# First attention's scores by pairs of heads, the products with the keys' remainder on 64 rows

## The chip, the core and the metric

One kernel launch on one core of a Trainium2 chip. The metric is the device time of one execution, in microseconds (us); times are medians of several runs, and the profile is of one further execution. PE is TensorE, PEld its weight loads, DVE is VectorE, ACT ScalarE, POOL GpSimd, SP SyncE, which only issues transfers here.

## What is computed

Two transformer blocks one after the other on 512 tokens of width 1024. The change touches the attention of the first block's second layer. It has 16 query heads of 64 columns, 4 key/value heads (so 4 query heads share one key head), a window of 128 tokens to either side, 256 context tokens that every query sees, and a sink logit. Cut to what matters:

```python
def block_fn(args):                       # one block of 128 queries
    i, qb = args
    kb = lax.dynamic_slice_in_dim(k_pad, i * BLOCK, 3 * BLOCK, axis=1)
    vb = lax.dynamic_slice_in_dim(v_pad, i * BLOCK, 3 * BLOCK, axis=1)
    ...
    s_band = jnp.einsum('bqhgd,bkhd->bhgqk', qb, kb)          # window, masked
    s_ctx = jnp.einsum('bqhgd,bkhd->bhgqk', qb, kc)           # context
    p = jax.nn.softmax(jnp.concatenate([s_band, s_ctx, s_sink_lat], axis=-1), axis=-1)
    o = einsum(p_band, vb) + einsum(p_ctx, vc)
```

Everything is float32. The kernel gets near it with matmuls in the type fp32r, which takes one pass where float32 takes two (a float32 matmul stands in the trace as two instructions): each operand is split into a rounded part ("hi", names ending in h) and the remainder ("lo", ending in l), and a product is the sum hi·hi + lo·hi + hi·lo.

## The kernel before

The program is built by a tile framework that gets the operations in the order in which the Python code emits them, with priorities, and runs a list scheduler over them: the order on each engine is the scheduler's, chosen by what it holds to be ready, not the order of emission. So a Python loop sets what there is to do and the dependences, and only loosely the order.

A linear layer (`mm3`, lines 155 to 165; L161, L163 and L165 are its three matmuls) loads 128x128 of the weights and streams up to 512 tokens. These are most of the run. The first attention (`attend`, `queries`, `wo`, from line 840) lies at 975 to 1174 us of 2372. Group g (0 to 3) is one key head with its four query heads, block b (0 to 3) is 128 queries; `attend(g, b)` is called 16 times. Between the calls stand the query projection of the next group (`queries`, L161 to L165 with xh, xl) and the output projection of the group before (`wo`, the same lines with oh, ol).

In `attend` each head i of the four does this:

- The stationary operand is q, 128 rows by 128 queries. A head has only 64 columns, so q holds the head twice: hi on one half of the rows and lo on the other. Even heads have hi on rows 0 to 63, odd heads on rows 64 to 127 (L856 writes hi, L859 computes lo, which a transfer moves to the other half). The keys' hi part kh[g] stands on both halves of the rows (L812 and a transfer), and so does the remainder kl[g] (L813).
- So one matmul q·kh (L887) gives hi·hi + lo·hi, and a second one, q·kl (L888), adds hi·lo and also lo·lo.
- The scores go to a PSUM tile `sc` of 1024 columns, of which there are two. There are two spans: the window's keys (384 columns for blocks 1 and 2, 256 for blocks 0 and 3) and the 256 of the context. So a head has four matmuls, and all heads 64 x 4 = 256: 128 on L887 and 128 on L888.
- DVE adds the mask and takes the maximum (L890), which frees the `sc` tile; ACT takes the exponential (L891); when all four heads are done DVE computes the reciprocal of the sum (L894 to L897) and POOL scales the rows (L899).
- For each block of 128 keys PE transposes the four heads' weights (L905, tile `aux`), ACT copies them (L907), and PE multiplies by the values (L909, tile `po`). L909 writes 64 partitions per matmul, two of them side by side in the array.

The form of a PE instruction in the trace gives the piece of the array that it uses, rows * columns: 128\*128 is the whole array, 128\*64 has half the columns (L909), 64\*128 half the rows.

Of the kernel before, what the change touches and what calls it, by code (L numbers as in the profile page):

```python
# [11 lines left out]
AF = mybir.ActivationFunctionType  # L12
ALU = mybir.AluOpType
# [44 lines left out]
def _build(ctx, tc, ins, out, stop, dbg):  # L58
    nc = tc.nc
    pe, act, dve, pool, sp = nc.tensor, nc.scalar, nc.vector, nc.gpsimd, nc.sync  # L60
# [8 lines left out]
    cur = B()  # L69
    cur.bufs, cur.tags, cur.done, cur.st = {}, {}, [0] * KT, None  # L70

    @contextmanager
    def sub(name, attr, side="left"):

        with tc.tile_pool(name=name, bufs=1, side=side, reuse_waits="tile") as p:
            old = getattr(cur, attr, None)
            setattr(cur, attr, p)
            yield
            setattr(cur, attr, old)

    @contextmanager
    def banks(name, **tags):

        with tc.tile_pool(name=name, bufs=1, space=PSUM, reuse_waits="tile") as p:
            old = cur.tags
            cur.tags = {t: list(l) for t, l in old.items()}
            for t, n in tags.items():
                cur.tags[t] = [(p, n)] * n + cur.tags.get(t, [])
            cur.turn = {}
            yield  # L90
            cur.tags = old

    def ps(cols=512, tag="mm", parts=128):
        n = cur.turn.get(tag, 0)
        cur.turn[tag] = n + 1
        p, bufs = cur.tags[tag][n % len(cur.tags[tag])]
        return p.tile([parts, cols], F32, tag=tag, bufs=bufs, name=tag)

    def wk(cols, tag, bufs=1, dt=F32, parts=128, first=False):

        p, bufs = cur.sm, cur.bufs.get(tag, bufs)
        if cur.st and tag in ("cv", "u"):
            n = cur.turn.get(tag, 0)
            cur.turn[tag] = n + 1
            p, bufs = (cur.st, 2) if first or n % bufs < 2 else (p, bufs - 2)
        return p.tile([parts, cols], dt, tag=tag, bufs=bufs, name=tag)
# [15 lines left out]
    def V(name, i=0, n=1):  # L122
        o, c = _VOFF[name]
        assert i + n <= c
        return vec[:, o + i : o + i + n]
# [4 lines left out]
    def load_unit(src, u, cols=2048):  # L130
        raw = cur.wp.tile([128, 2048], F32, tag="raw", bufs=cur.raw, name="raw")
        sp.dma_start(out=raw[:, :cols], in_=src[u][:, :cols])
        return raw

    def split_w(raw, h, p=None):
        part = raw[:, h * 1024 : (h + 1) * 1024]
        cur.nw += 1
        if p is None and cur.early_w and cur.nw % (cur.w + 1) == 0:
            p = cur.wa
        p, n = (cur.wp, cur.w) if p is None else (p, 1)  # L140
        hi = p.tile([128, 1024], F32R, tag="wh", bufs=n, name="wh")
        lo = p.tile([128, 1024], F32R, tag="wl", bufs=n, name="wl")
        act.activation(out=hi, in_=part, func=AF.Copy)  # L143
        dve.tensor_tensor(out=lo, in0=part, in1=hi, op=ALU.subtract)  # L144
        return hi, lo
# [9 lines left out]
    def mm3(pieces, w, xs, first, last, mcol):  # L155

        whi, wlo = w
        xhi, xlo = xs
        c = slice(mcol, mcol + 128)
        for p, s in pieces:  # L160
            pe.matmul(p, whi[:, c], xhi[:, s], start=first, stop=False)  # L161
        for p, s in pieces:
            pe.matmul(p, whi[:, c], xlo[:, s], start=False, stop=False)  # L163
        for p, s in pieces:
            pe.matmul(p, wlo[:, c], xhi[:, s], start=False, stop=last)  # L165
# [268 lines left out]
    with sub("a_x", "xp"), sub("a_w", "wp"), sub("a_s", "sm"):  # L434
# [13 lines left out]
        for k in range(KT):  # L448
            q = wk(TOK, "prod", 2)
# [11 lines left out]
        r = wk(8, "rs", 2)  # L461
# [303 lines left out]
    kh = [wk(TOK, f"kh{g}", dt=F32R) for g in range(4)]  # L765
    kl = [wk(TOK, f"kl{g}", dt=F32R) for g in range(4)]
# [5 lines left out]
    nsink = wk(16, "nsink")  # L772
# [67 lines left out]
    qs, ob, qp = {}, {}, [cur.sm, None]  # L840
# [32 lines left out]
    with sub("c_b", "oa"), sub("c_a", "sm", "right"), banks("c_p1", mm=1), banks("c_p2", sc=2), banks("c_p0", po=1), banks("c_p3", aux=2):  # L873
        qp[1] = cur.sm
        def attend(g, b):
            blocks = [t for t in (b - 1, b, b + 1) if 0 <= t < 4]
            nb = 128 * len(blocks)
            W = nb + 256
            mk = mask[:, 0:640] if len(blocks) == 3 else mask[:, 128:640] if b == 0 else mask[:, 640:1152]
            c = slice(b * 128, (b + 1) * 128)  # L880
            n4, l4 = wk(4, "n4", 3), wk(4, "l4", 3)
            P = []
            for i in range(4):
                q = qs[4 * g + i][:, c]
                sc = ps(1024, tag="sc")
                for dst, src in ((sc[:, 512 - nb : 512], slice(blocks[0] * 128, blocks[0] * 128 + nb)), (sc[:, 512:768], slice(512, 768))):
                    pe.matmul(dst, q, kh[g][:, src], start=True, stop=False)  # L887
                    cur.mark = pe.matmul(dst, q, kl[g][:, src], start=False, stop=True)  # L888
                s = wk(640, "s", 8)
                dve.tensor_tensor_reduce(out=s[:, :W], in0=sc[:, 512 - nb : 768], in1=mk, scale=1.0, scalar=nsink[:, 4 * g + i : 4 * g + i + 1], op0=ALU.add, op1=ALU.min, accum_out=n4[:, i : i + 1])  # L890
                act.activation(out=s[:, :W], in_=s[:, :W], func=AF.Exp, scale=-1.0, bias=n4[:, i : i + 1], accum_out=l4[:, i : i + 1])  # L891
                P.append(s)
            e4 = wk(4, "e4", 3)
            dve.tensor_tensor(out=e4, in0=V("sink1", 4 * g, 4), in1=n4, op=ALU.add)  # L894
            act.activation(out=e4, in_=e4, func=AF.Exp)
            dve.tensor_tensor(out=l4, in0=l4, in1=e4, op=ALU.add)
            dve.reciprocal(out=l4, in_=l4)  # L897
            for i in range(4):
                pool.tensor_tensor(out=P[i][:, :W], in0=P[i][:, :W], in1=l4[:, i : i + 1].to_broadcast([128, W]), op=ALU.mult)  # L899
            po = ps(256, tag="po")  # L900
            keys = blocks + [4, 5]
            for n, t in enumerate(keys):
                pt = ps(512, tag="aux")
                for i in range(4):
                    pe.transpose(pt[:, i * 128 : (i + 1) * 128], P[i // 2 + i % 2 * 2][:, n * 128 : (n + 1) * 128], ident)  # L905
                p = wk(512, "p", 3)
                act.copy(out=p, in_=pt)  # L907
                for e in range(2):
                    pe.matmul(po[64 * e : 64 * e + 64], va[:, t, g], p[:, 256 * e : 256 * e + 256], start=n == 0, stop=n == len(keys) - 1)  # L909
            if b == 0:  # L910
                ob[g] = [cur.oa.tile([128, 1024], F32R, tag=n, bufs=3, name=n).rearrange("p (j t) -> p j t", j=2) for n in ("oh", "ol")]
            o = po.rearrange("p (j t) -> p j t", j=2)
            oh, ol = [x[:, :, c] for x in ob[g]]
            act.activation(out=oh, in_=o, func=AF.Copy)
            dve.tensor_tensor(out=ol, in0=o, in1=oh, op=ALU.subtract)

        def wo(g, cols=512, tags=("mm",)):
            raw = load_unit(ins["wo"], g)
            ws = [split_w(raw, 0), split_w(raw, 1)]
            for c0 in range(0, 512, cols):  # L920
                for m in range(KT):
                    t = tags[m % len(tags)]
                    p = (ps(512) if t == "mm" else ps(1024, tag="sc"))[:, 0:cols]
                    for i in range(2):
                        mm3([(p, slice(c0, c0 + cols))], ws[i], [x[:, i] for x in ob[g]], i == 0, i == 1, m * 128)
                    dve.scalar_tensor_tensor(out=hl[m][:, c0 : c0 + cols], in0=p, scalar=mod[1][:, 16 + m, 0:1], in1=hl[m][:, c0 : c0 + cols], op0=ALU.mult, op1=ALU.add)
                    cur.done[m] = tc.cur_priority

        for g in range(4):
            for b in range(4):  # L930
                attend(g, b)
                if b == QB and g < 3:
                    queries(g + 1)
                if (g, b) in WOP:
                    with tc.issue_after(cur.mark.ins) if WOI else ExitStack():
                        wo(WOP.index((g, b)))
        wo(3, 256, ("sc", "mm", "sc"))
# [151 lines left out]
    bias = wa(6 * 256, "bias").rearrange("p (h j) -> p h j", h=6)  # L1089
# [182 lines left out]
    with sub("e_x", "xp"), sub("e_w", "wp"), sub("e_t", "sm"):  # L1272
# [34 lines left out]
        for n, (name, i) in enumerate(order):  # L1307
# [12 lines left out]
            if name in ("l", "r", "k", "v"):  # L1320
                shifted(u, {"r": 0, "k": 3, "v": 6, "l": 9}[name] + i, lora if name == "l" else rkv[name][i])
                if n == PREPN:
# [8 lines left out]
                    m4k, eye64, pair = rc[0], rc[1][:, 0:64], rc[1][:, 64:192]  # L1331
# [384 lines left out]
```

## Time and profile before

| | |
|---|---|
| median of 3 runs | 2374.22 us (2371.76 to 2375.54) |
| the profiled execution | 2373.74 us, its span 2372.0 us |
| mean granted TensorE clock | 0.987 |
| PE busy | 2279.0 us, 96% of the span |
| DVE, ACT, POOL busy | 69%, 40%, 7% |
| first attention (975 to 1163 us): PE busy | 178.6 of 188 us |
| its score matmuls L887 and L888 | 256 instructions |

A matmul's duration in the trace includes its passage through the array, which lies over the next matmul's; so what a matmul costs in a row of matmuls is read from start to start, and the busy time of a group is more than what it costs. Where a row says x2 or x4, consecutive instructions of one kind are merged.

### The profile page before, as it was taken

The page shows a single profiled execution, that of the slowest core. Times are in us where ns is not written, and L with a number is a line of the kernel's source. Part 1 is how long each engine was busy: PE and PEld are TensorE (multiplying, and loading weights), DVE is VectorE, ACT ScalarE, POOL GpSimd, SP SyncE. Part 2 cuts the span into 40 slices and gives each one's busy share as a digit, 9 for nine tenths or more (in the row PEclk, how much of TensorE's full clock was granted, in tenths as well). Part 3 has the DMA queues.
Part 4 walks back from the last instruction along what each step waited for, and adds up shares of the span by engine and source line. Part 5 has one row for each costly group of instructions (what it writes and reads, how often), then busy time and mean ns, then how long its engine had stood idle before and what let it go on. Part 6 is the DMA issues. An engine that isn't in the chain of part 4 may idle for free.

```text
span 2372.0 us, 34287 instructions
## 1 busy us (share of the span) xinstructions
PE 2279.0 (96%) x13910; PEld 1885.8 (80%) x13910; DVE 1644.5 (69%) x2634; ACT 942.7 (40%) x1616; POOL 170.9 (7%) x246
## 2 busy tenths in 40 slices
PE   5999899999999999899999999998989999999999
PEld 2777588888888888766789999987768786788887
DVE  4889769867677768666687777676645546767666
ACT  3222633223332235566653433355633323433332
POOL 0000000000000000344300000001431100000000
PEclk8999999999999999999999999999999999999999
DMA  8455323323233211421132322222200002232221
GB/s 314 168 206 172 139 115 116 124 99 107 90 128 112 98 54 55 129 68 36 54 118 78 124 74 106 72 73 68 66 23 23 5 28 105 87 106 90 89 89 54
DMA packets 51385, 229.02 MB, mean 97 GB/s; under 512 B 6395, under 2 KB 11164, under 8 KB 32796
## 3 DMA queue, kind: packets, MB, share of 16 engines
q1 hardware_dynamic: 51228, 226.84, 27.8%
q8 instruction: 109, 1.79, 0.3%
q14 instruction: 48, 0.39, 0.1%
HBM read 213.84 MB, written 6.68 MB: 93 GB/s over the span
## 4 chain that ended last, share of the span: by engine, by line
PE 88%; DVE 5%; ACT 3%; DMA 2%; issue 1%; POOL 0%; SPq 0%; DVEq 0%; ACTq 0%; POOLq 0%
PE mm L161 23%; PE mm L163 23%; PE mm L165 23%; PE po L909 1%; PE aux L905 1%; PE mm L576 1%; PE rw L1436 1%; PE rw L1430 1%; PE rw L1424 1%; DMA raw<-in_ada 1%; PE aux L370 1%; PE sc L887 1%; PE mm L783 1%; PE sc L888 1%; PE aux L402 1%
## 5 line engine op out<-in xcount | busy, mean ns | idle before, releaser
L161 PE MATMUL mm<-xh,wh 128*128 128x512 f32 (+2 forms) x2336 | 658.4, 338 | 15.2 <-ACT xh L479 4.7
L163 PE MATMUL mm<-xl,wh 128*128 128x512 f32 (+2 forms) x2336 | 660.9, 337 | 3.1 <-DVE xl L219 2.1
L165 PE MATMUL mm<-xh,wl 128*128 128x512 f32 (+2 forms) x2336 | 659.7, 337 | 1.9 <-DVE wl L144 1.9
L143 ACT ACTIVATE wh<-raw 128x1024 fp32r<-128x1024 f32 x263 | 274.8, 1057 | 543.3 <-PE mm L163 491.9
L161 PEld LDWEIGHTS mm<-xh,wh 128*128 128x128 f32 x2336 | 409.5, 190 | 70.5 <-ACT xh L479 6.8
L163 PEld LDWEIGHTS mm<-xl,wh 128*128 128x128 f32 x2336 | 410.8, 190 | 55.5 <-DVE xl L219 3.1
L165 PEld LDWEIGHTS mm<-xh,wl 128*128 128x128 f32 x2336 | 410.7, 190 | 49.2 <-DVE wl L144 2.8
L144 DVE TENSOR_TENSOR wl<-raw,wh 128x1024 fp32r<-128x1024 f32 x263 | 324.2, 1242 | 44.5 <-ACT wh L143 40.0
L161 PE MATMUL mm<-gh,wh 128*128 128x512 f32 (+1 forms) x704 | 253.7, 368 | 2.2 <-ACT gh L288 2.0
L163 PE MATMUL mm<-gl,wh 128*128 128x512 f32 (+1 forms) x704 | 254.8, 368 | 0.0
L165 PE MATMUL mm<-gh,wl 128*128 128x512 f32 x704 | 254.0, 367 | 0.0
L249 DVE TENSOR_TENSOR u<-mm,R 128x256 f32<-128x256 f32 x88 | 37.5, 426 | 178.5 <-PE mm L165 176.7
L161 PEld LDWEIGHTS mm<-gh,wh 128*128 128x128 f32 x704 | 131.3, 188 | 26.1 <-ACT gh L288 2.4
L165 PEld LDWEIGHTS mm<-gh,wl 128*128 128x128 f32 x704 | 131.3, 189 | 23.4
L163 PEld LDWEIGHTS mm<-gl,wh 128*128 128x128 f32 x704 | 131.3, 189 | 23.0 <-DVE gl L289 0.3
L310 DVE SCALAR_TENSOR_TENSOR hl<-mm,mod,hl 128x512 f32<-128x512 f32 x176 | 131.3, 747 | 21.1 <-PE mm L165 20.5
L288 ACT ACTIVATE gh<-cv 128x512 fp32r<-128x512 f32 (+1 forms) x66 | 46.5, 705 | 243.0 <-DVE cv L286 243.0
L271 DVE SCALAR_TENSOR_TENSOR cv<-u,vec,cv 128x512 f32<-128x512 f32 (+1 forms) x132 | 110.4, 837 | 9.9 <-ACT cv L262 9.2
L553 DVE SCALAR_TENSOR_TENSOR accp<-v,dwt,accp 128x798 f32<-128x798 f32 (+2 forms) x118 | 113.9, 975 | 2.6
L272 DVE SCALAR_TENSOR_TENSOR cv<-u,vec,cv 128x512 f32<-128x512 f32 (+1 forms) x132 | 110.6, 839 | 3.1
L284 ACT ACTIVATE cv<-cv 128x512 f32<-128x512 f32 (+1 forms) x66 | 46.4, 704 | 118.2 <-DVE cv L272 118.0
L396 DVE SCALAR_TENSOR_TENSOR ac<-ra,sc,ac 128x512 f32<-128x512 f32 x112 | 81.8, 744 | 1.4 <-DMA ra<-in_ada 1.4
(470 smaller groups left out, 3092.2 us busy)
## 6 DMA issues: line engine op xcount, KB each, us to landing
raw<-in_up SPq DMA_DIRECT2D x63, 1024.0 KB, 4.9
raw<-in_dn SPq DMA_DIRECT2D x33, 1024.0 KB, 4.8
raw<-in_ada SPq DMA_DIRECT2D x24, 1024.0 KB, 6.3
ra<-in_ada SPq DMA_DIRECT2D x48, 512.0 KB, 3.6
raw<-in_pw SPq DMA_DIRECT2D x12, 1024.0 KB, 6.2
S<-vd SPq DMA_DIRECT2D x28, 407.0 KB, 5.0
raw<-in_w_in SPq DMA_DIRECT2D x17, 512.0 KB, 3.5
raw<-in_qkv SPq DMA_DIRECT2D x6, 1024.0 KB, 5.0
```

The lines of the kernel that those rows point to most:

```text
L143: act.activation(out=hi, in_=part, func=AF.Copy)
L144: dve.tensor_tensor(out=lo, in0=part, in1=hi, op=ALU.subtract)
L161: pe.matmul(p, whi[:, c], xhi[:, s], start=first, stop=False)
L163: pe.matmul(p, whi[:, c], xlo[:, s], start=False, stop=False)
L165: pe.matmul(p, wlo[:, c], xhi[:, s], start=False, stop=last)
L271: dve.scalar_tensor_tensor(out=cv[:, 0:CW], in0=u[:, 0:CW], scalar=wv[0], in1=cv[:, 0:CW], op0=ALU.mult, op1=ALU.add)
L272: dve.scalar_tensor_tensor(out=cv[:, 0:CW], in0=u[:, 2 : 2 + CW], scalar=wv[2], in1=cv[:, 0:CW], op0=ALU.mult, op1=ALU.add)
L284: act.activation(out=ca[:, 0:CW], in_=ca[:, 0:CW], func=AF.Silu)
L288: act.activation(out=gh[:, 0:CW], in_=cb[:, 0:CW], func=AF.Copy)
L310: dve.scalar_tensor_tensor(out=hs, in0=p, scalar=g2[i][:, m : m + 1], in1=hs, op0=ALU.mult, op1=ALU.add)
L396: dve.scalar_tensor_tensor(out=a, in0=t[:, q, :], scalar=sc2[:, k, n : n + 1], in1=a, op0=ALU.mult, op1=ALU.add)
L553: dve.scalar_tensor_tensor(out=acc[:, a:b], in0=x, scalar=w, in1=acc[:, a:b], op0=ALU.mult, op1=ALU.add)
```

## The change

The heads are taken by pairs (0, 1) and (2, 3). For a pair, the code emits the four matmuls with kh as before, over all 128 rows. Then it emits the four with kl, span by span, the two heads' alternately, and each takes only the 64 rows on which its own hi part lies: rows 0 to 63 for the even head, 64 to 127 for the odd one. The number of matmuls, their columns, the weight loads and the tiles stay as they were; the product lo·lo is no longer added. Then the two heads' evictions and exponentials follow.

```diff
-            for i in range(4):
-                q = qs[4 * g + i][:, c]
-                sc = ps(1024, tag="sc")
-                for dst, src in ((sc[:, 512 - nb : 512], slice(blocks[0] * 128, blocks[0] * 128 + nb)), (sc[:, 512:768], slice(512, 768))):
-                    pe.matmul(dst, q, kh[g][:, src], start=True, stop=False)
-                    cur.mark = pe.matmul(dst, q, kl[g][:, src], start=False, stop=True)
-                s = wk(640, "s", 8)
...
+            for i0 in (0, 2):
+
+                pair = [(i, qs[4 * g + i][:, c], ps(1024, tag="sc")) for i in (i0, i0 + 1)]
+                spans = ((slice(512 - nb, 512), slice(blocks[0] * 128, blocks[0] * 128 + nb)), (slice(512, 768), slice(512, 768)))
+                for i, q, sc in pair:
+                    for dst, src in spans:
+                        pe.matmul(sc[:, dst], q, kh[g][:, src], start=True, stop=False)
+                for dst, src in spans:
+                    for i, q, sc in pair:
+                        r = slice(64 * (i % 2), 64 * (i % 2) + 64)
+                        cur.mark = pe.matmul(sc[:, dst], q[r], kl[g][r, src], start=False, stop=True)
+                for i, q, sc in pair:
+                    s = wk(640, "s", 8)
...
```

Behind it every line number is 6 higher: L887 becomes L889, L888 becomes L893, L905 becomes L911 and L909 becomes L915.

Where the two heads' products end up on PE is the scheduler's doing. The first pair of the stage (group 0, block 0), after the change (L889 are the products with kh, L893 those with kl; sc_8450 is the even head's tile, sc_8451 the odd head's):

```order
5039 L889 MATMUL sc_8450<-kh0_7876,qs_8272 128x256 x2
5040 L889 MATMUL sc_8451<-kh0_7876,qs_8273 128x256 x2
5041 L893 MATMUL sc_8450<-kl0_7880,qs_8272 128x256
5042 L893 MATMUL sc_8451<-kl0_7880,qs_8273 128x256
5043 L893 MATMUL sc_8450<-kl0_7880,qs_8272 128x256
5044 L893 MATMUL sc_8451<-kl0_7880,qs_8273 128x256
```

The two heads stand alternately, as emitted. The second pair is alternate in part. From there on, the third pair (group 0, block 1) and all others stand like this, with other work between the heads or none:

```order
5077 L889 MATMUL sc_8534<-kh0_7876,qs_8272 128x384
5078 L889 MATMUL sc_8534<-kh0_7876,qs_8272 128x256
5079 L893 MATMUL sc_8534<-kl0_7880,qs_8272 128x384
5080 L893 MATMUL sc_8534<-kl0_7880,qs_8272 128x256
5081 L889 MATMUL sc_8535<-kh0_7876,qs_8273 128x384
5082 L889 MATMUL sc_8535<-kh0_7876,qs_8273 128x256
5083 L893 MATMUL sc_8535<-kl0_7880,qs_8273 128x384
5084 L893 MATMUL sc_8535<-kl0_7880,qs_8273 128x256
```

Each head's four matmuls stand together: two on all rows, two on 64. A pair late in the stage (group 3, block 1), on PE before the change, from the even head to the odd head:

```order
5680 L887 MATMUL sc_9862<-kh3_7879,qs_9557 128x256
5681 L888 MATMUL sc_9862<-kl3_7883,qs_9557 128x256
5682 L887 MATMUL sc_9862<-kh3_7879,qs_9557 128x256
5683 L888 MATMUL sc_9862<-kl3_7883,qs_9557 128x256
5684 L909 MATMUL po_9730<-p_9736,va_7884 64x256 x2
5685 L909 MATMUL po_9730<-p_9745,va_7884 64x256 x2
5686 L905 MATMUL aux_9758<-ident_66,s_9694 128x128
5687 L905 MATMUL aux_9758<-ident_66,s_9710 128x128
5688 L905 MATMUL aux_9758<-ident_66,s_9702 128x128
5689 L905 MATMUL aux_9758<-ident_66,s_9718 128x128
5690 L887 MATMUL sc_9870<-kh3_7879,qs_9558 128x256
```

and the same pair after it:

```order
5630 L889 MATMUL sc_9862<-kh3_7879,qs_9557 128x256 x2
5631 L893 MATMUL sc_9862<-kl3_7883,qs_9557 128x256 x2
5632 L911 MATMUL aux_9731<-ident_66,s_9718 128x128
5633 L911 MATMUL aux_9740<-ident_66,s_9718 128x128
5634 L889 MATMUL sc_9863<-kh3_7879,qs_9558 128x256 x2
5635 L893 MATMUL sc_9863<-kl3_7883,qs_9558 128x256 x2
5636 L161 MATMUL mm_10101<-oh_8974,wh_10037 128x512
```

Here too the heads stand apart, and two transposes have come between them. Over the whole stage the 128 products on L893 stand in 63 runs: 60 of two (one head's two spans), and one each of one, three and four. In 5 places a product stands next to one on the other 64 rows. The places on PE where the piece of the array changes from one instruction to the next are 122 in this stage before and 227 after. Outside the first attention the order moves only in the second block's attention, where scores, transposes and projections are interleaved in another way.

## Rows read from the trace of the kernel before

**Rows 1.** The page: busy time by engine, and the chain that ended last.
```profile
PE 2279.0 (96%) x13910; PEld 1885.8 (80%) x13910; DVE 1644.5 (69%) x2634; ACT 942.7 (40%) x1616; POOL 170.9 (7%) x246
...
PE 88%; DVE 5%; ACT 3%; DMA 2%; issue 1%; POOL 0%; SPq 0%; DVEq 0%; ACTq 0%; POOLq 0%
```

**Rows 2.** Windows: stretch, us, each engine's busy us, granted clock, DMA share.
```profile
975.00:1010.00 35.00, 30.57 (x151) 24.24 (x150) 24.23 (x42) 20.84 (x40) 16.89 (x11) 0.95 0.33 92
1010.00:1088.00 78.00, 73.06 (x454) 51.23 (x454) 51.79 (x110) 51.96 (x115) 36.70 (x31) 1.00 0.25 72
1088.00:1163.00 75.00, 74.97 (x468) 52.18 (x468) 43.15 (x103) 47.87 (x108) 34.15 (x31) 1.00 0.02 8
```

**Rows 3.** Line 888: count, ns min/median/max, first and last start, forms.
```profile
L888 PE MATMUL sc<-kl,qs x128: 274/281/366, 975.6 to 1155.9; 128*128 128x256 f32 x96, 128*128 128x384 f32 x32
```

**Rows 4.** Timeline of PE in the stage: start us, duration us, line, form.
```profile
1015.78 0.34 PE L887 MATMUL sc<-kh,qs 128*128 128x384 f32 x1
1015.95 0.34 PE L888 MATMUL sc<-kl,qs 128*128 128x384 f32 x1
1016.12 0.28 PE L887 MATMUL sc<-kh,qs 128*128 128x256 f32 x1
1016.24 0.28 PE L888 MATMUL sc<-kl,qs 128*128 128x256 f32 x1
```

**Rows 5.** Timeline of the weight loads: that of the matmul at 1015.95.
```profile
1015.78 0.19 PEld L888 LDWEIGHTS sc<-kl,qs 128*128 128x128 f32 x1
```

**Rows 6.** Timeline of PE: from the whole array to 32 of its rows.
```profile
1684.52 0.39 PE L165 MATMUL mm<-xh,wl 128*128 128x512 f32 x1
1684.84 1.12 PE L1212 MATMUL aux<-lora,lw 32*128 32x512 f32 x2
```

**Rows 7.** Lines 1512 (64 rows) and 1496 (whole array), and their timelines.
```profile
L1512 PE MATMUL mm<-lora,lw x6: 589/641/693, 1864.4 to 1970.9; 64*128 64x512 f32 x6
...
L1496 PE MATMUL mm<-f,rc x6: 592/594/697, 1863.3 to 1969.9; 128*128 128x512 f32 x6
...
1932.19 1.02 PE L1496 MATMUL mm<-f,rc 128*128 128x512 f32 x2
...
1864.94 0.59 PE L1512 MATMUL mm<-lora,lw 64*128 64x512 f32 x1
1865.45 1.16 PE L1430 MATMUL rw<-T,XT 128*128 128x128 f32 x8
```

**Rows 8.** Timeline of PE: the first matmuls behind a change to the whole array.
```profile
1774.67 0.50 PE L161 MATMUL wo<-oh,wh 128*128 128x512 f32 x1
1775.01 0.40 PE L163 MATMUL wo<-ol,wh 128*128 128x512 f32 x1
1775.24 0.39 PE L165 MATMUL wo<-oh,wl 128*128 128x512 f32 x1
```

**Rows 9.** Timeline of PE: value products and transposes, in eights and in fours.
```profile
1013.22 1.08 PE L909 MATMUL po<-p,va 128*64 128x256 f32 x8
1014.24 1.09 PE L905 MATMUL aux<-ident,s 128*128 128x128 f32 x8
...
1017.62 0.65 PE L909 MATMUL po<-p,va 128*64 128x256 f32 x4
1018.20 0.66 PE L905 MATMUL aux<-ident,s 128*128 128x128 f32 x4
1018.79 0.65 PE L909 MATMUL po<-p,va 128*64 128x256 f32 x4
```

**Rows 10.** Waits of PE, 975 to 1163 us: us in total, times, longest.
```profile
PE sc L887 <- DVE n L890: 4.1, 4, 2.3
PE mm L161 <- ACT qu L850: 3.2, 1, 3.2
```

**Rows 11.** Windows of the second block's attention, columns as in rows 2.
```profile
1600.00:1690.00 90.00, 83.87 (x403) 62.08 (x402) 55.12 (x107) 57.22 (x107) 17.02 (x31) 0.96 0.21 69
1690.00:1770.00 80.00, 73.88 (x398) 54.50 (x397) 43.78 (x121) 36.72 (x99) 32.72 (x47) 0.94 0.13 38
```

More of the change, by code (lines that the diff above doesn't have):

```diff
@@ L882, in attend @@
             P = []
-            for i in range(4):
-                q = qs[4 * g + i][:, c]
-                sc = ps(1024, tag="sc")
-                for dst, src in ((sc[:, 512 - nb : 512], slice(blocks[0] * 128, blocks[0] * 128 + nb)), (sc[:, 512:768], slice(512, 768))):
-                    pe.matmul(dst, q, kh[g][:, src], start=True, stop=False)
-                    cur.mark = pe.matmul(dst, q, kl[g][:, src], start=False, stop=True)
-                s = wk(640, "s", 8)
-                dve.tensor_tensor_reduce(out=s[:, :W], in0=sc[:, 512 - nb : 768], in1=mk, scale=1.0, scalar=nsink[:, 4 * g + i : 4 * g + i + 1], op0=ALU.add, op1=ALU.min, accum_out=n4[:, i : i + 1])
-                act.activation(out=s[:, :W], in_=s[:, :W], func=AF.Exp, scale=-1.0, bias=n4[:, i : i + 1], accum_out=l4[:, i : i + 1])
-                P.append(s)
+            for i0 in (0, 2):
[10 more added lines that the diff above has]
+                    s = wk(640, "s", 8)
+                    dve.tensor_tensor_reduce(out=s[:, :W], in0=sc[:, 512 - nb : 768], in1=mk, scale=1.0, scalar=nsink[:, 4 * g + i : 4 * g + i + 1], op0=ALU.add, op1=ALU.min, accum_out=n4[:, i : i + 1])
+                    act.activation(out=s[:, :W], in_=s[:, :W], func=AF.Exp, scale=-1.0, bias=n4[:, i : i + 1], accum_out=l4[:, i : i + 1])
+                    P.append(s)
             e4 = wk(4, "e4", 3)
```

## The prediction, made before the changed kernel was run

> **What bounds the kernel now.** I read the page first [rows 1]: PE is busy for 96% of the span, and 88% of the chain that ended last is PE's. So the question is whether the change shortens PE's own work in the first attention, and whether PE is the bound there too. The windows by stretch answer the second [rows 2]: over 975 to 1163 us PE is busy for 178.6 of 188 us (30.57 + 73.06 + 74.97), DVE for 119, ACT for 121, POOL for 88. In the last 75 us PE has no gap at all. What lengthens PE's work there lengthens the run. Of the 9.4 us in which it idles, all but 0.03 lie before 1088 us, and its waits [rows 10] say on whom: 3.2 us once on a query eviction at the very start, 4.1 us on score tiles that DVE had not yet freed.
>
> Then I read what a score product costs. The group's own row [rows 3] gives 281 ns for the median of the 128 products with the remainder, but this contains the passage through the array. From start to start [rows 4] it is 0.17 us for 384 columns (1015.78 to 1015.95 and on to 1016.12) and 0.12 us for 256 (1016.12 to 1016.24). The weight load of the product at 1015.95 starts at 1015.78, while the matmul before it runs [rows 5]: in a row of equal array pieces, loads cost nothing.
>
> **What the change could save.** Two matmuls on different halves of the rows could run side by side. If all 32 pairs did, one of each two remainder products would vanish: 16 pairs of blocks 1 and 2 at 0.17 + 0.12 us, 16 of blocks 0 and 3 at 0.12 + 0.12, together 4.6 + 3.8 = 8.5 us. But the order on PE gives this to two pairs only. With two score tiles in all, the odd head's tile is seldom free when the even head's is, and the scheduler then finishes the even head. In 5 places a remainder product follows one on the other half of the rows; in one run of four and one of three that is at most three products of 256 columns out of the way: 3 x 0.12 = **0.4 us saved**. I take it whole, since nothing here shows two such neighbours in fp32r; the other end is 0.
>
> The other 123 or so products stay one after the other. Half the rows do not shorten a matmul: 64 rows by 512 columns [rows 7] take 589 ns at the least, on the whole array 592 [rows 7]. I take equal durations. That fp32r on 64 rows would run at float32's pace is not shown by any row and excluded by none; its price would be large (0.43 us per 512 columns against 0.23 [rows 8], so about twice the 128 products' 17 us), and I leave it out of the range.
>
> **What the change adds.** A change of the array piece costs PE time, in two parts, and both are in the trace.
>
> - The wait before it. In the projections one matmul of 512 columns follows the other by 0.23 us (1775.01 to 1775.24 [rows 8]), but the step from such a one to 32 rows is 0.32 us [rows 6]: **0.09 us** more. Out of 64 rows it is 1864.94 to 1865.45, 0.51 us; two such passes on the whole array last 1.02 us from 1932.19 on, of which the second's own 0.59 leaves 0.43 from start to start [rows 7]: 0.08 more.
> - The first matmul behind it, whose weights are not loaded ahead. On 64 rows the first takes 693 ns and the second 589 [rows 7]: **0.10 us**. Back on the whole array the first step is 0.34 us (1774.67 to 1775.01), the next 0.23 [rows 8]: **0.11 us**.
>
> So a change costs 0.195 us into 64 rows and 0.2 us out of them to a matmul with 128 columns of weights. Between value products and transposes it is cheaper [rows 9]: eight instead of four lengthen a run by 0.43 us (1.08 and 1.09 us against 0.65 and 0.66), yet a run of four followed by the other kind takes 0.58 to 0.59 us from start to start (1017.62, 1018.20, 1018.79): 0.15 us per change.
>
> The order has 227 such places in this stage where it had 122. Of them, by what comes behind: 63 lead into the 64 rows, at 0.195 = 12.3 us; those into whole-array matmuls rise from 5 to 32, 27 x 0.195 = 5.3 us; those into transposes from 56 to 72, 16 x 0.15 = 2.4 us; those into value products fall from 61 to 60, -0.15 us. Together **+19.9 us** of PE time, 105 changes at 0.19 us each. All are PE's own time in a stage that PE bounds.
>
> [...]
>
> **What hides some of it.** Other work is no cover, since the extra time is on PE. But PE's waits shrink when PE comes later. The 3.2 us wait lies before all but the first pair and stays. Of the other 6.2 us, waits for DVE, ACT and POOL before 1088 us, I take half: **-3 us** (ends 0 and -6.2). DVE's, ACT's and POOL's own work does not change, and each product reaches DVE in the same order as before, one head at a time; no wait is added on them.
>
> **The rest.** The scheduler also moves work in the second block's attention. PE idles there for 6.1 us in each of two stretches and its clock is granted at 0.96 and 0.94 [rows 11]. What the new interleaving does there I cannot work out from rows; I take 0, with 4 us to either side (a third of the 12.2 us idle).
>
> **The sum.** 2373.74 (the profiled execution: span 2372.0 and 1.7 around it) + 19.9 - 0.4 - 3 = 2390.2. The median of the runs shown lies 0.5 us above that execution, so 2390.7; I say **2390.5 us**, 16 us or 0.7% slower. Under about 0.2% (4.7 us) a measurement of this kernel cannot tell a difference from none.
>
> **Rivals.**
>
> - *The load is hidden, only the drain is paid.* If the loads for 64 rows can run beside the last whole-array matmul, a change costs 0.09 us: 105 x 0.09 = 9.5, less 3.4, gives 2380. For it: halves of rows are loaded by instructions of their own. Against it: line 1512, which also goes from the whole array to 64 rows, has its 0.10 us [rows 7]. Chance 0.08, in which slower and no difference are about equal.
> - *The second span's load is exposed as well.* The two products of a head lie on the same 64 rows. If a load could be made ahead only for other rows than those at work, each run of two would pay another 0.10 us: 62 x 0.104 = 6.4 us, 2397. Against it: the second pass of line 1512, on the same rows as the first, has no such 0.10 us [rows 7], and on the whole array the load runs ahead [rows 5]. Chance 0.06. [...]
> - *Half the rows count as the same piece.* All 128 columns stay in use, so the array might not have to be emptied, and nothing but the 0.4 us moves: 2373.8. Against it: rows 6 and 7 also keep all 128 columns and show both parts. Chance 0.05, no difference.
> - *Faster: the new order fills PE's waits.* With more, smaller independent pieces of score work, PE would no longer stand still before 1088 us. This gives at most 9.4 us, so it decides only if a change costs under 9.4 / 105 = 0.09 us, less than the drain alone; with changes at nothing it gives 2374.2 - 9.4 - 0.4 = 2364.4. For it: scores and projections of that stretch are interleaved anew. Against it: 75 of the 188 us have no wait to fill [rows 2]. Chance 0.05.
>
> **How the numbers follow.** My forecast has 0.76. Its own range comes from the ends above: 2390.5 - 3.2 (all waits filled) - 4 = 2383 and 2390.5 + 3 + 4 + 0.4 = 2398. With the two other slower cases the range is **2380 to 2400 us**; outside lie the last two rivals and little more. Slower by over 0.2%: 0.76 + 0.04 + 0.06, 0.86. Within 0.2%: 0.05 + 0.04, 0.09. Faster: 0.05.
>
> **What would show it.** In the timeline after the change, a head's first product with the remainder should start about 0.21 us (256 columns) behind its last product with kh instead of 0.12, and its own step should be longer by 0.10 us; what follows should start 0.09 us late. PE should have no more idle time in the stage than before, and the stage should end some 16 us later. The two products of one head should stand 0.12 or 0.17 us apart. Wrong I am if steps into and out of the 64 rows are as short as without a change, or if the stage's length grows without PE being busy, which would be a wait that I have not seen.

## The result, and the profile after

The changed kernel takes **2390.47 us** (median of 6 runs, 2383.92 to 2392.97), the kernel before 2374.68 us (6 runs, 2371.76 to 2375.54): 1.0064 times the time, with an interval of 1.0050 to 1.0078. It is slower by about 16 us, where 2390.5 us was forecast. The profiled execution is the lowest of the six, 2383.92 us with a span of 2382.1 us.

The page of the kernel after; the rows answer to [rows 1]:

```profile
PE 2296.4 (96%) x13910; PEld 1888.0 (79%) x13910; DVE 1649.7 (69%) x2634; ACT 941.3 (40%) x1614; POOL 172.5 (7%) x246
...
PE 90%; DVE 5%; DMA 2%; ACT 2%; issue 1%; SPq 0%; POOL 0%; DVEq 0%; ACTq 0%; POOLq 0%
```

PE has the same 13910 instructions and is busy for 17.4 us more (2296.4 against 2279.0); its part of the chain that ended last grows from 88% to 90%. DVE, ACT and POOL are nearly where they were.

Windows of the kernel after, columns and stretches as in [rows 2]:

```profile
975.00:1010.00 35.00, 32.73 (x151) 23.32 (x152) 23.24 (x44) 21.70 (x44) 15.03 (x11) 0.95 0.30 78
1010.00:1088.00 78.00, 77.33 (x440) 51.04 (x442) 52.23 (x104) 51.31 (x111) 35.23 (x27) 1.00 0.24 69
1088.00:1163.00 75.00, 74.19 (x415) 47.29 (x415) 41.25 (x95) 41.74 (x96) 32.64 (x28) 1.00 0.03 10
```

In the last stretch PE is as busy as before (74.19 against 74.97 us of 75) and gets through 415 matmuls instead of 468. In the middle one its idle time falls from 4.9 us to 0.7, and it still gets through fewer. So the time did not go into a wait: the matmuls of these stretches take more of PE's time. The stretches do not hold quite the same work in both kernels; the window of the whole stage, below, does.

The timeline of PE after the change, late in the stage (start us, duration us, line, form; L889 are the products with kh, L893 those with kl, L911 the transposes):

```profile
1129.33 0.48 PE L889 MATMUL sc<-kh,qs 128*128 128x256 f32 x2
1129.74 0.51 PE L893 MATMUL sc<-kl,qs 64*128 64x256 f32 x2
1130.17 0.66 PE L911 MATMUL aux<-ident,s 128*128 128x128 f32 x4
1130.58 0.48 PE L889 MATMUL sc<-kh,qs 128*128 128x256 f32 x2
1131.00 0.50 PE L893 MATMUL sc<-kl,qs 64*128 64x256 f32 x2
```

One head's score work and four transposes take 1129.33 to 1130.58, 1.25 us: 0.41 for the two products on all rows, 0.43 for the two on 64, 0.41 for the transposes. The first experiment gives the same piece of work without a change of the array piece.

The weight loads of the second head in those rows:

```profile
1130.67 0.19 PEld L889 LDWEIGHTS sc<-kh,qs 128*128 128x128 f32 x1
1131.00 0.29 PEld L893 LDWEIGHTS sc<-kl,qs 64*128 64x128 f32 x2
```

The first load for the 64 rows starts at 1131.00, with its own matmul; in [rows 5] the load started 0.17 us ahead of its matmul. Two loads of 0.183 us (the median of L893's loads) stand in 0.29 us, so the second starts near 1131.11, some 0.12 us ahead of the second product on the same rows. It is so in the whole stage: all 63 first loads for 64 rows start within 2 ns of their own matmul, where the same loads start 114 ns ahead (median) in the first experiment, which has this order on all rows.

Last, the stage itself. In the rest of this document the *stage* is the stretch from the first score product to the last product with the values. Its window in the kernel before:

```profile
975.40:1173.90 198.50, 188.84 (x1145) 135.14 (x1143) 124.57 (x263) 123.67 (x267) 87.40 (x71) 0.99 0.17 50
```

and in the kernel after:

```profile
972.10:1182.40 210.30, 205.25 (x1145) 135.97 (x1143) 127.91 (x263) 124.95 (x267) 88.11 (x71) 0.99 0.16 47
```

PE's waits in that window (us in total, times, longest):

```profile
PE mm L161 <- ACT qu L850: 3.3, 2, 3.0
PE po L915 <- ACT p L913: 0.9, 2, 0.6
PE sc L889 <- DVE n L896: 0.7, 1, 0.7
```

For the same 1145 matmuls PE is busy for 16.4 us more and idle for 4.6 us less (5.05 against 9.66, length less busy time), so the stage is 11.8 us longer. The waits say what is left of the idle time: the wait for score tiles, 4.1 us in [rows 10], is down to 0.7 us, the one on the query eviction at the start stands.

The granted clock is the same in both windows (0.99). The stage does not hold the whole 16 us. Where the rest lies, and whose it is (the 64 rows', or the new order's), the profile after cannot tell. That was the first question to the chip.

### The profile page after: what moved, and what is told of

The parts are those of the page before. It is cut to its first block, busy times and chain, and to the rows that moved or that the text cites. A ratio compares the mean times of both kernels' runs of the same rounds, so it can differ in the third digit from the quotient of the medians.

```text
span 2382.1 us, 34270 instructions
## 1 busy us (share of the span) xinstructions
PE 2296.4 (96%) x13910; PEld 1888.0 (79%) x13910; DVE 1649.7 (69%) x2634; ACT 941.3 (40%) x1614; POOL 172.5 (7%) x246
## 4 chain that ended last, share of the span: by engine, by line
PE 90%; DVE 5%; DMA 2%; ACT 2%; issue 1%; SPq 0%; POOL 0%; DVEq 0%; ACTq 0%; POOLq 0%
PE mm L161 23%; PE mm L163 23%; PE mm L165 23%; PE aux L911 2%; PE po L915 2%; PE mm L576 1%; PE rw L1442 1%; PE sc L893 1%; PE rw L1436 1%; PE rw L1430 1%; PE sc L889 1%; DMA raw<-in_ada 1%; PE aux L370 1%; PE mm L783 1%; PE mm L1404 1%
## 5 line engine op out<-in xcount | busy, mean ns | idle before, releaser
L143 ACT ACTIVATE wh<-raw 128x1024 fp32r<-128x1024 f32 x263 | 274.6, 1057 | 533.9 <-PE mm L163 484.2
L905 POOL TENSOR_TENSOR s<-s,l 128x512 f32<-128x512 f32 (+1 forms) x64 | 77.2, 1237 | 91.2 <-DVE l L903 83.2
```

## The experiments

**The theory** was that of the prediction: every change between the whole array and 64 of its rows costs PE 0.15 to 0.2 us, the 64 rows bring some 105 more of them, and hardly any products run side by side, because the scheduler puts a head's products together. **The rivals**: that the new order costs the time, whatever the rows (other interleaving in the stage and in the second block's attention); that only the wait of 0.09 us is paid per change; and that half rows would gain if the alternation survived.

The first four kernels ran in one session, in which the kernel before had a median of 2376.39 us (17 runs), the last two in another, where it had 2373.05 us (17 runs). Ratios are against the kernel before in the same session.

### The new order on all rows

The changed kernel with one line altered; PE's order, and that of every other engine, is the changed kernel's, instruction for instruction. The lo·lo product is added as in the kernel before.

```diff
-                        r = slice(64 * (i % 2), 64 * (i % 2) + 64)
+                        r = slice(0, 128)
```

> The kernel after the change with the products with the remainder on all 128 rows again; every engine's order of instructions is the one after the change. It separates the 64 rows from the new order. My theory (the changes of the array piece cost 0.19 us each, 105 of them, less the waits that they fill): the loss is gone and the time is 2368 to 2376 us. Rival (the new order and its waits cost the time, not the 64 rows): it stays at 2385 to 2391 us.

Measured: 2375.61 us (12 runs, 2372.13 to 2383.26), ratio 0.9999 [0.9990, 1.0009]. The loss is gone, so it comes with the 64 rows and not with the order. Window of its stage:

```profile
974.70:1169.80 195.10, 187.65 (x1145) 133.88 (x1143) 129.05 (x263) 124.14 (x267) 88.37 (x71) 0.99 0.18 51
```

Timeline of PE, the same piece of work as above:

```profile
1120.16 0.48 PE L889 MATMUL sc<-kh,qs 128*128 128x256 f32 x2
1120.48 0.40 PE L893 MATMUL sc<-kl,qs 128*128 128x256 f32 x2
1120.72 0.60 PE L911 MATMUL aux<-ident,s 128*128 128x128 f32 x4
1121.08 0.37 PE L889 MATMUL sc<-kh,qs 128*128 128x256 f32 x1
```

Two products on all rows, two with the remainder, four transposes: 0.32, 0.24 and 0.36 us, 0.92 in all, against 0.41, 0.43 and 0.41 us with 64 rows. The differences are 0.09 us ahead of the change (the wait before it), 0.19 us within (the load that is not ahead, 0.10, and the wait on the way out, 0.09) and 0.05 us behind it. Two changes cost 0.33 us; the prediction's prices for them are 0.195 + 0.15 = 0.345.

Over the stage the 64 rows bring 107 more changes in this same order (234 against 127, counted in the two traces; for the kernels before and after the traces give 129 and 234, 7 more each than the text on the change, and only differences are used here). PE is busy for 17.6 us more than here (205.25 less 187.65) and idle for 2.4 us less (5.05 against 7.45): 15.2 us.

The 1145 PE instructions are the same in both traces, one for one, so the steps from start to start can be set side by side. By them 18.4 us of PE's time go to the changes and 3.2 us come back from shorter waits. The changes cost 0.09 us ahead of the first product with kl (63 places), 0.10 us before the second (62), and, where transposes or matmuls of the whole array follow (44), some 0.08 us on the way out and 0.05 to 0.10 us for the first load behind it. The 19 ways out to value products cost nothing more (205 ns against 209, medians): with all rows the piece changes there too. That is 0.17 us for each of the 107.

Against the kernel before the new order alone makes the stage 3.4 us *shorter* (195.1 against 198.5). This does not show in the whole time.

### Twice the changes in the old order

The kernel before, with the remainder's product on 64 rows and nothing else. There it stands alone between two products on all rows, so each one pays its way in and out: 363 changes in the stage instead of 129, counted in the traces. It too leaves out lo·lo.

```diff
-                    cur.mark = pe.matmul(dst, q, kl[g][:, src], start=False, stop=True)
+                    r = slice(64 * (i % 2), 64 * (i % 2) + 64)
+                    cur.mark = pe.matmul(dst, q[r], kl[g][r, src], start=False, stop=True)
```

> The kernel before with the products with the remainder on 64 rows and nothing else changed; every engine's order is the one before, so the products with kh and kl take turns one by one and the array's piece changes 352 times in the stage where it changed 118 times. It more than doubles the suspected cost without the new order. My theory (0.19 us per change): 234 more changes add 45 us to PE, 3 to 6 us of it in PE's waits: 2412 to 2420 us. Rival (only the wait of 0.09 us before a change is paid): 234 x 0.09 = 21 us, less the same: 2389 to 2394 us. Rival (the order costs, not the changes): 2374 us as before.

Measured: 2415.40 us (4 runs, 2411.74 to 2418.29), ratio 1.0165 [1.0151, 1.0178]. Window of its stage:

```profile
976.30:1212.40 236.10, 233.57 (x1145) 146.34 (x1144) 123.41 (x262) 125.17 (x267) 84.06 (x71) 0.98 0.14 42
```

Timeline of PE, one head (here L887 are the products with kh, L889 those with kl):

```profile
1100.61 0.38 PE L887 MATMUL sc<-kh,qs 128*128 128x256 f32 x1
1100.92 0.38 PE L889 MATMUL sc<-kl,qs 64*128 64x256 f32 x1
1101.23 0.38 PE L887 MATMUL sc<-kh,qs 128*128 128x256 f32 x1
1101.55 0.38 PE L889 MATMUL sc<-kl,qs 64*128 64x256 f32 x1
1101.86 0.65 PE L910 MATMUL po<-p,va 128*64 128x256 f32 x4
```

Every step is 0.31 us where [rows 4] has 0.12 us for the same columns. PE's busy time in the stage grows by 44.7 us (233.57 less 188.84) for 234 more changes, 0.191 us each. But part of it is the clock's. The granted clock of this stage is 0.98, the kernel before's 0.99, and the difference lies in one stretch, here at half of full speed (granted clock 0.50):

```profile
1057.40:1067.60 10.20, 10.20 (x24) 6.49 (x24) 2.21 (x7) 1.02 (x3) 7.26 (x8) 0.50 0.00 0
```

PE had been busy for all of the ten us before it (1047 to 1057). The kernel before has 3.4 us at that level in its stage. The steps in question are longer by some 2.6 us in all than the same steps and changes at full speed; without them it is 42.1 us, **0.18 us each**, a little under the 0.19 at which the prediction bought them. PE's idle time falls from 9.7 to 2.5 us, so the waits do shrink when PE comes later, and by more the more PE is delayed.

### The alternation forced

The changed kernel, with a bracket by which the four products with kl are emitted as one piece behind the pair's last product with kh. PE then has them as the change's text says: over the stage 95 of 95 neighbouring products lie on different halves, in 33 runs, and the changes of the array piece fall from 234 to 183.

```diff
-                        pe.matmul(sc[:, dst], q, kh[g][:, src], start=True, stop=False)
-                for dst, src in spans:
-                    for i, q, sc in pair:
-                        r = slice(64 * (i % 2), 64 * (i % 2) + 64)
-                        cur.mark = pe.matmul(sc[:, dst], q[r], kl[g][r, src], start=False, stop=True)
+                        lead = pe.matmul(sc[:, dst], q, kh[g][:, src], start=True, stop=False)
+                with tc.issue_after(lead.ins):
+                    for dst, src in spans:
+                        for i, q, sc in pair:
+                            r = slice(64 * (i % 2), 64 * (i % 2) + 64)
+                            cur.mark = pe.matmul(sc[:, dst], q[r], kl[g][r, src], start=False, stop=True)
```

> The kernel after the change with the four products with the remainder of each pair forced behind the pair's last product with kh, so that the two heads do stand alternately on PE: 33 runs, 95 of 95 neighbours on different halves of the rows, 176 changes of the array piece in the stage against 118 before. My theory: 58 more changes at 0.19 us cost 11 us, 62 to 64 products side by side with another save 8.5 us, so the stage is 2 to 3 us longer than the same order with 128 rows, plus what waiting for both score tiles costs: 2374 to 2386 us. Rival (products in fp32r on different halves do not run side by side): 8 us more than that, 2383 to 2394 us, and the starts of a run of four lie 0.12 us apart each.

Measured: 2389.33 us (5 runs, 2385.21 to 2391.43), ratio 1.0055 [1.0043, 1.0067]. This missed: it is above the expected range, and no better than the scheduler's order. Timeline of PE, one pair (here L894 are the products with kl):

```profile
1104.32 0.83 PE L889 MATMUL sc<-kh,qs 128*128 128x384 f32 x4
1105.08 0.56 PE L894 MATMUL sc<-kl,qs 64*128 64x384 f32 x4
1105.56 0.66 PE L912 MATMUL aux<-ident,s 128*128 128x128 f32 x4
1105.97 0.48 PE L161 MATMUL mm<-oh,wh 128*128 128x512 f32 x1
```

Window of the stage:

```profile
972.20:1176.50 204.30, 193.34 (x1151) 128.72 (x1150) 125.91 (x264) 123.79 (x267) 87.36 (x71) 0.98 0.16 45
```

The wait for score tiles in it:

```profile
PE sc L889 <- DVE n L897: 3.8, 4, 2.4
```

The products do run side by side: the records of the two halves start at most 4 ns apart. Four products with kl (two of 384, two of 256 columns) take 0.48 us. That is one 384 and one 256, 0.29 us, plus 0.19 us for the load and the way out. The stage is 6 us shorter than with the scheduler's order (204.3 against 210.3), yet the whole time is not, and PE waits for score tiles again (3.8 us). Was this a second cost of the 64 rows, or of the order that the bracket forces? That needed the same order on all rows.

### The kernel after once more

No edit; a second profile of the changed kernel, to see what of the time between stages repeats.

> The kernel after the change once more, for a second profile and more times. The profiled execution was 2383.9 us, the median 2390.5. My theory of that difference: in the longer executions TensorE's granted clock is at half for more stretches (mean 0.981 against 0.985); expected a time near 2390 us with a mean clock near 0.981 and more or longer half-clock stretches in the trace. Rival: the same clock and a stage whose waits differ from execution to execution.

Measured: 2390.50 us (6 runs, 2385.71 to 2393.17), ratio 1.0057 [1.0045, 1.0069]. The profiled execution took 2393.17 us, 9.3 us more than the one above, for the same program. Windows of this one (before the stage, the stage, from it to the second block's attention):

```profile
0.00:970.00 970.00, 925.95 (x5641) 762.60 (x5642) 720.89 (x1082) 329.21 (x566) 5.38 (x14) 0.98 0.37 130
978.20:1189.10 210.90, 205.22 (x1145) 135.97 (x1143) 129.25 (x263) 124.93 (x267) 88.60 (x71) 0.99 0.16 47
1189.10:1636.80 447.70, 442.70 (x3001) 408.66 (x2999) 331.14 (x542) 198.91 (x313) 0.00 (x0) 0.99 0.28 97
```

and the same parts of the first profile, without the stage:

```profile
0.00:970.00 970.00, 924.98 (x5678) 766.01 (x5679) 725.79 (x1088) 332.34 (x572) 5.54 (x14) 0.99 0.38 132
...
1182.40:1627.60 445.20, 439.75 (x3001) 406.41 (x3000) 330.96 (x542) 198.94 (x313) 0.00 (x0) 1.00 0.28 97
```

The stage repeats within 0.6 us. The rest does not: by 970 us PE has got through 5641 matmuls here and 5678 there, the stage starts at 978.2 instead of 972.1 us, and the stretch behind it takes 2.5 us more, each at a lower granted clock. The stretches at half of full speed (granted clock 0.50) add up to 93.1 us here and to 69.3 us in the first profile. So a single profile cannot settle a few us outside the stage; the stage's own window can be compared from run to run, and for the whole the medians.

### The forced alternation on all rows

The third experiment's kernel with `r = slice(0, 128)`, its order the same on every engine; lo·lo is added as before.

```diff
-                            r = slice(64 * (i % 2), 64 * (i % 2) + 64)
+                            r = slice(0, 128)
```

> The forced alternate order with the products with the remainder on all 128 rows; every engine's order is that of the forced kernel on 64 rows (2389.3 us, score stage 204.1 us from the first score to the last value product). It separates, in that kernel, what 58 more changes of the array piece cost and what 62 to 64 products side by side save from what the forced order costs. My theory: changes cost 11 us, side by side saves 8 us, so this one is 2 to 4 us shorter, 2385 to 2388 us, with a stage of 200 to 203 us; the rest of the 13 us above the kernel before is the order's. Rival (the changes cost, and nothing is saved since the products don't really overlap): 11 us shorter, 2376 to 2380 us. Rival (the overlap gains more than the changes cost): longer than 2389 us.

Measured: 2386.37 us (6 runs, 2384.30 to 2387.40), ratio 1.0053 [1.0039, 1.0066]. Timeline of PE, the same piece of work:

```profile
1106.67 0.83 PE L889 MATMUL sc<-kh,qs 128*128 128x384 f32 x4
1107.33 0.74 PE L894 MATMUL sc<-kl,qs 128*128 128x384 f32 x4
1107.91 0.60 PE L912 MATMUL aux<-ident,s 128*128 128x128 f32 x4
1108.27 0.48 PE L161 MATMUL mm<-oh,wh 128*128 128x512 f32 x1
```

Windows of the stage, and of two stretches behind the second block's attention:

```profile
977.50:1178.00 200.50, 189.67 (x1151) 134.63 (x1149) 126.47 (x264) 123.65 (x267) 86.94 (x71) 0.99 0.16 46
...
1970.00:1980.00 10.00, 6.06 (x82) 4.17 (x76) 3.35 (x10) 1.19 (x2) 0.00 (x0) 0.81 0.09 28
1980.00:1990.00 10.00, 9.66 (x28) 5.48 (x28) 2.68 (x6) 0.92 (x3) 0.00 (x0) 0.67 0.00 0
```

Four products with kh, four with kl and four transposes take 0.66, 0.58 and 0.36 us, 1.60 in all; on 64 rows and side by side it was 0.76, 0.48 and 0.41 us, **1.65**. The overlap saves 0.29 us of a pair's 0.58, and the two changes take 0.10 + 0.19 + 0.05 = 0.34 us. Over the stage that is 3.8 us against the 64 rows (204.3 against 200.5; PE busy for 3.67 us more), but not all of it is theirs: the stage on 64 rows has a second stretch at half of full speed (1046.3 to 1049.7 us, clock 0.98 against 0.99), whose steps are 1.6 us longer. Some 2 us are left, 0.07 us for each of 32 pairs. By their medians the two kernels lie 3.0 us apart; but they ran in different sessions, and their ratios to the kernel before, 1.0055 and 1.0053, can't be told apart. So that perfect alternation loses rests on the stage and the pair, not on the whole time.

Most of what both lose, some 13 us, is the forced order's. Little of it lies in the stage (200.5 us against the kernel before's 198.5). From the end of the second block's attention on, both take 625.4 us, the kernel after 620.3, and the kernel before 617.4 and, in a second profile (the last experiment), 620.6. So 5 to 8 us lie there; the rest of the 13 is not placed. The last two windows say where the 5 to 8 us are: PE is busy for 6.06 us of ten, and the granted clock is low there and in the ten that follow. The same windows of the kernel after:

```profile
1970.00:1980.00 10.00, 7.55 (x119) 5.74 (x118) 3.79 (x11) 1.46 (x3) 0.00 (x0) 1.00 0.09 29
1980.00:1990.00 10.00, 9.14 (x40) 6.06 (x39) 6.06 (x10) 1.53 (x3) 0.00 (x0) 1.00 0.00 0
```

and its timeline of DVE there (in brackets the idle time before, and who ended it):

```profile
1974.97 0.28 DVE L1486 SCALAR_TENSOR_TENSOR f<-aux,lend,f 128x64 f32<-128x64 f32 x1 [0.44 <-PE aux L1485]
1975.89 0.69 DVE L1553 TENSOR_TENSOR NM<-NM 128x512 fp32r<-128x512 f32 x1 [0.64 <-ACT NM L1552]
```

The timelines of DVE, then of PE, in the forced order on all rows:

```profile
1971.40 0.28 DVE L1487 SCALAR_TENSOR_TENSOR f<-aux,lend,f 128x64 f32<-128x64 f32 x1 [0.36 <-PE aux L1486]
1973.75 0.69 DVE L1554 TENSOR_TENSOR NM<-NM 128x512 fp32r<-128x512 f32 x1 [2.06 <-ACT NM L1553]
1974.35 0.28 DVE L1487 SCALAR_TENSOR_TENSOR f<-aux,lend,f 128x64 f32<-128x64 f32 x1
...
1974.69 0.33 PE L1486 MATMUL aux<-f 64*64 64x64 f32 x4 [2.50 <-DVE f L1487]
```

NM and f are tiles of a later part of the program. In the forced order the scheduler has put the operation on NM two small steps (f) earlier on DVE than in the kernels before and after. DVE then stands 2.06 us before it, waiting for ACT; the small step behind it is held up, and PE waits 2.50 us for that one. Behind this gap the clock is at its lower level, half of full speed, for 10.2 us: two passes of 512 columns (L1503) take 2.07 us in it, where [rows 7] has 1.02 for the same two. The wait and half of that stretch are 7.6 us, an estimate that lies at the upper end of what this part has grown by. By it one operation on DVE that moved ahead of two others, 800 us behind the edit, cost more than the forced order does in the stage (2.0 us). Both forced kernels have the DVE operation at this place and such a stretch behind it (from 1974.8 us on 64 rows, from 1976.3 us on all), and none of the other profiles has a stretch at the lower clock there; that the clock fell because of the gap was not tried by itself.

### The kernel before once more

No edit.

> The kernel before once more, for a second trace. My theory: the stretches in which two executions of one kernel differ lie outside the score stage (the start, up to 975 us, by where the half-clock stretches fall); the stage from the first score to the last value product is again 198 us within 1 us, and the part behind the second block's attention again 617 us within 1 us. Rival: the stage itself varies by several us, and then its differences between kernels say little.

Measured: 2375.25 us (8 runs, 2373.39 to 2377.94), ratio 1.0009 [0.9999, 1.0020]. Its stage, and from the second block's attention's end to the end:

```profile
972.50:1170.50 198.00, 188.84 (x1145) 135.13 (x1143) 125.14 (x263) 123.61 (x267) 87.56 (x71) 0.99 0.17 50
1751.90:2372.50 620.60, 598.23 (x3462) 486.34 (x3460) 386.34 (x550) 206.31 (x284) 34.30 (x96) 0.98 0.19 66
```

The stage repeats (198.0 and 198.5 us, PE busy for 188.84 us both times). The last part does not: the first profile has

```profile
1754.60:2372.00 617.40, 594.29 (x3462) 483.56 (x3460) 386.21 (x550) 206.30 (x284) 34.37 (x96) 0.99 0.19 67
```

and the kernel after has 620.3 us. About 617 us was expected here; the 3 us that this part seemed to lose by the change thus come and go with the granted clock in the same program.

## Why the prediction was right

**The bound.** PE was the bound in the stage and stayed it: with 107 changes more than on all rows it is busy for 205.25 of 210.3 us. The stage grew with PE busy, not with a wait. Of the signs named beforehand the steps came as forecast and PE's idle time did not grow; but the stage became 11.8 us longer, not 16.

**The price of a change.** It is right in its two parts and nearly in size: 0.33 us measured for a pair of changes priced at 0.345; as a mean 0.17 us for each of the 107 of the first experiment and 0.18 us for each of the 234 of the second, where 0.19 was forecast. The single records of the kernel after say the same of 256 columns: from the last product with kh to the first with kl 209 ns (median) where it is 118 ns on all rows, and from this one to the second with kl 223 ns instead of 118; 91 and 105 ns against the 0.09 and 0.10 us forecast.

**The sum.** The forecast for the stage was +19.9 - 0.4 = 19.5 us of PE work and -3 us of waits. Measured against the kernel before: 16.4 us of busy time and -4.6 us of waits, 11.8 in place of 16.5. What the sum did not have is the effect of the new order by itself: on all rows it shortens the stage by 3.4 us, 2.2 us of it idle time (7.45 us in place of 9.66) and 1.2 us busy time. Against that same order the terms nearly fit: the 64 rows bring 18.4 us of PE work, for 19.5 forecast, and 3.2 us come back from waits, for 3 forecast, 15.2 us in all. That waits give back 3 us was no more than the middle of a range.

**The rest**, taken as 0 with 4 us to either side. The medians differ by 16 us and the stages by 12 to 13, so some 3 to 4 us lie outside the stage. They do not come with the 64 rows: in one session the kernel after (2390.50 us) and its order on all rows (2375.61 us) differ by 14.9 us, and their stages by as much (15.2 us, 15.8 with the second profile). The order gives back outside the stage what it saves in it: on all rows the whole time is that of the kernel before (interval 0.9990 to 1.0009) although the stage is 3.4 us shorter. Where it does so is open, since the profiles of one program differ by as much there. The second block's attention itself did not grow (134.2 us after, 134.0 before, by its windows). So the cost of the 64 rows was worked out, but that the point forecast met the median within 0.1 us is luck: the order's two effects, neither in the sum, nearly cancel, and so do the smaller errors, among them PE work forecast 1 us too high.

**The rivals.** *Only the drain*, the prediction's word for the wait of 0.09 us before a change: falls, each change pays the load too (0.10 us within the pair, 0.05 us behind it into transposes). *The second span's load exposed as well*: falls; the second product's load starts ahead of it, by 114 to 179 ns in the 62 places, and the step behind that product carries no more than the way out. *Half rows count as the same piece*: falls with the 0.31 us steps. *Faster, the new order fills PE's waits*: the order does take waits away, 2.2 us, but a change costs twice the 0.09 us at which this could have decided.

**The saving.** Two products on different halves ran side by side in fp32r here: in the first pair of the kernel after, their records start 3 and 4 ns apart. What was credited (0.4 us for the few places) agrees with the first pair, whose four products of 256 columns take 0.44 us to the next instruction (972.65 to 973.09): 2 x 0.12 + 0.10 + 0.09. What the prediction put at 8.5 us for all pairs would have been had, and would not have been enough.

No kernel here beats the one before. The new order on all rows is the best of the variants and equals it.

## What to carry to other kernels

Before splitting the rows of the array between two products, price the way in and out: here two changes cost 0.33 us and the overlap saved 0.24 to 0.29 us per pair of heads, so even perfect alternation lost; whether longer runs on the same rows turn that was not tried. Under a list scheduler look at the order on the engine, not at the loops: alternate emission gave alternate products for one of 32 pairs and in part for a second, and a bracket that forced it moved an operation on another engine, 800 us behind the edit, by the estimate above at more cost than in the stage itself. Judge a change of this size by medians and by the window of its own stage, which repeated within 0.6 us where the whole varied by 9; and look at the granted clock of both windows first, since a stretch at half of full speed that only one of them had made up 1.6 and 2.6 us of two differences here.

## What was not expected of the hardware

Two profiles of the changed kernel, the same program, differ by 9.3 us (2383.92 and 2393.17 us), with stretches at half of full speed of 69.3 and 93.1 us in all. The higher clock did not come with a busier PE: from 240 to 270 us it is busy for 22.89 us of 30 in the first and 23.41 in the second, and the granted clock is 1.00 and 0.83. And the second product on 64 rows paid nothing for its load, which starts 114 to 179 ns ahead, although it lies on the very rows that are at work: 105 ns more for the first step, and none for the next but the wait on leaving.
